# Seven products for eight in one more outgoing step of a split-precision feed-forward block

## The chip, the cores and the metric

The kernel runs on one core of a Trainium2 chip. Its time is that of one execution on the device, in microseconds (us), and the median of several executions is quoted. Numerical work is in float32. TensorE multiplies in a shortened float format (fp32r), so each factor is split into a high and a low part, and one product in full precision is three matmuls: high by high, high by low, low by high.

## The reference

One layer of a hybrid encoder on 512 tokens (T) of width 1024, from one conditioning vector c:

```python
x += 1/2 * g1 * SwiGLU_1(mod(RMSNorm(x)))
x += g2 * W_out( sig(gA) * W_A(WindowGQA+sink) + sig(gB) * W_B(DiffAttn) )
x += 1/2 * g3 * SwiGLU_2(mod(RMSNorm(x)))

def swiglu(h, w_in, w_out):
    gate, up = jnp.split(h @ w_in, 2, axis=-1)
    return (jax.nn.silu(gate) * up) @ w_out
```

The shifts, scales and gates (mod and g) are nine vectors of 1024, which come from c by the matrix w_mod (1024 by 9216). The hidden width of a SwiGLU is 2816, which is 22 chunks of 128. The first block ("first SwiGLU") is the one that the change touches most.

## The kernel before

The token axis lies along the free dimension, in two halves of 256; a chunk is 128 hidden units. Hidden chunks go in pairs, 0 to 10.

The first block's pairs 0 to 2 are computed by plain products. Each pair from 3 on is a `Unit` (u3 to u10): a 2x2 block product done with seven smaller products in place of eight, s1, s2, s3, s4, a11, a12 and a22. The weights' sums for that are formed on their way in, by transfers which GpSimd's queue adds to what lies in the buffer (`G.dma_start(..., accum_op=ALU.add)`); the sums of results are formed by VectorE and ScalarE from the PSUM banks, in `Unit.after`. A product of a unit is four steps deep, 24 matmuls of 256 columns, in `two` (L458 to L460). After s2, s1 and a11 a ScalarE COPY (L536) takes the bank out; the products that go on in that bank wait for it.

The outgoing product of the first block (hidden to model width) runs in four groups of chunks, `CHUNKS`: 0 to 6, 6 to 12, 12 to 16 and 16 to 22. Each is an `Out1`: eight rows, one for each 128 of the model width, and a row is (chunks in the group) x 3 matmuls of 512 columns in `mm3` (L174 to L176). After each row VectorE adds it to the residual x with the gate (L947, x_78 to x_85). Each row needs one weight load on SP's queue (`raw<-w1o`), and one split: a ScalarE CAST to the high part and a VectorE subtraction to the low part (both L190, `split_from`).

Between products the list `items1` places other work. `side1` runs modulation columns, one for each credit of 1.0, with 0.27 credited for each item: such a column is a load of 512 KB into one half of the buffer `room` (`b<-w_mod`) and a VectorE multiply-and-sum (L283, `b<-b,ka`). The second SwiGLU has its outgoing products done by sevens already (`act_split`, `out_unit`, with products of 18 matmuls of 256 columns in three parts of the depth): for that, the activations of a pair are also summed and split into seven operands.

Work on SP's and GpSimd's queues stands in the order of the program; PE, VectorE and ScalarE run in the order in which a list scheduler put them, and each engine takes its instructions strictly in turn. `tc.issue_after(i)` keeps an instruction behind i, `tc.high_priority()` moves one forward in that list.

After the first block come rows of constants (`row`: gains, lambda vectors, sinks), from which the rotary tables (L1104 to L1107), the lambda sums (L1088) and the sink copy are made, and then the mixer's norm: the last four rows of the final `Out1` are added (L947, then by token halves in L381), squared on ScalarE (L304), summed (L310) and reduced by small matmuls (`tp<-ones,f`, L343).

In the mixer's end the merged value is split to two parts for its outgoing product. The second SwiGLU begins with the unit `Plain`, whose gating is at L1765 to L1772.

Of the kernel before, what the change touches and what calls it, by code (L numbers as in the profile page):

```python
# [18 lines left out]
P = 128  # L19
# [93 lines left out]
EARLY, NEXT, SIDE, LATER = 3, 3, 0.27, 4  # L113
# [21 lines left out]
def layer(ctx: ExitStack, tc: tile.TileContext, a: dict):  # L135
# [326 lines left out]
    class Unit:  # L462
# [13 lines left out]
        asked, length = ("s1", "a11", "a12", "a22"), 1.0  # L476

        in_order, by_columns, asides = (), (), {}
# [148 lines left out]
    with tc.manual_schedule(engines=BOUND | {mybir.EngineType.SP, mybir.EngineType.Pool}):  # L627
# [246 lines left out]
    def in_post1(c, v, u):  # L874

        if c[1] == "1":
            u.v["g" + c[2]] = v
            S.activation(v, v, AF.Silu)
            if "c2" + c[2] in u.v:
                in_post1("c2" + c[2], u.v["c2" + c[2]], u)  # L880
            return
        if "g" + c[2] not in u.v:
            u.v[c] = v
            return
        g = u.v["g" + c[2]]
        V.scalar_tensor_tensor(g, g, -1.0, v, ALU.mult, ALU.mult)
        t, r = act_of(u.p), HALVES[int(c[2]) - 1]
        split_from(t[:, 0:2, r], t[:, 2:4, r], g.rearrange("p (j q) -> p j q", j=2))

    def in_unit1(p):  # L890
        srcs = {q: a["w1u"][p - PLAIN, i] for i, q in enumerate(("a11", "a12", "a21", "a22"))}
        u = Unit(srcs, 4, h1_operand, in_post1, p % 2)
        u.p, u.in_order = p, ('s2', 's4')
        if p == PLAIN:
            u.asides = {"s1": FIRST}
        elif 2 * p in [c.start for c in CHUNKS[1:]] or p == PLAIN + 1:
            u.asides = {"s2": FIRST}
        return u

# [54 lines left out]
    def item1(u, q, ks=None):  # L954
        items1.append((u, q, ks, side1))
# [15 lines left out]
    def side1(n=SIDE):  # L971
# [8 lines left out]
    with tc.manual_schedule(engines={mybir.EngineType.SP, mybir.EngineType.Pool}):  # L980
# [25 lines left out]
        begun = PLAIN  # L1006
        for n, chunks in enumerate(CHUNKS):


            final = n + 1 == len(CHUNKS)  # L1010
            for p in range(begun, max(chunks.stop // 2, PLAIN + 1)):
                u, nxt = units1[p], units1.get(p + 1)
                if p == PLAIN:
                    item1(u, "s1")
                    item1(u, "a11")
                elif p > begun:
                    item1(units1[p - 1], "a22")
                if p == PLAIN or p > begun:
                    item1(u, "a12")
                item1(u, "s2")  # L1020
                if nxt:
                    item1(nxt, "s1")
                item1(u, "s3")
                item1(u, "s4")
                if nxt:
                    item1(nxt, "a11")
            item1(u, "a22")
            if nxt:
                item1(nxt, "a12")
            begun, nxt = p + 1, nxt or u  # L1030
            out = Out1(chunks, "acc" if nxt.odd != final else "sc", final)
            if final:
                first = range(len(chunks) - 2)
                for m in range(2):
                    item1(out, m, first)
                for m in range(2):
                    item1(out, m, range(len(chunks) - 2, len(chunks)))
            for m in range(2 if final else 0, NC - LAST_1 if final else NC):
                item1(out, m)
# [9 lines left out]

    V.tensor_scalar(sub8, par[:, SUBLN : SUBLN + 1], 1.0 - LAM_INIT, None, ALU.mult)  # L1050
# [34 lines left out]
    lam_p = f2()[:, 0 : 2 * HD].rearrange("p (i d) -> p i d", i=2)  # L1085
    for i in range(2):
        o = ROW_LAM + 2 * i * HD
        V.tensor_tensor_reduce(  # L1088
            out=lam_p[:, i, :], in0=row[:, o : o + HD], in1=row[:, o + HD : o + 2 * HD],
            scale=1.0, scalar=0.0, op0=ALU.mult, op1=ALU.add, accum_out=lam_s[:, i : i + 1],  # L1090
        )
# [8 lines left out]
    for nm, o in (("qa", ROW_QA), ("ka", ROW_KA), ("qb", ROW_QB), ("kb", ROW_KB)):  # L1100
# [3 lines left out]
        V.tensor_tensor(C[:, :, 0:NF], cos_t, g0, ALU.mult)  # L1104
        V.tensor_tensor(C[:, :, NF:HD], cos_t, g1, ALU.mult)
        V.scalar_tensor_tensor(R[:, :, 0:NF], sin_t, -1.0, g1, ALU.mult, ALU.mult)
        V.tensor_tensor(R[:, :, NF:HD], sin_t, g0, ALU.mult)  # L1107
# [4 lines left out]
    V.tensor_copy(  # L1112
        sink.rearrange("p (g k) -> p k g", k=2), row[:, ROW_SINK : ROW_SINK + 8].rearrange("p (k g) -> p k g", k=2)
    )
# [575 lines left out]
    def main():  # L1690
# [24 lines left out]
        def then_b(j, g, y, r):  # L1715
# [3 lines left out]
            split_from(mh[j][:, r], ml[j][:, r], m)  # L1719
# [59 lines left out]
    act = {}  # L1779

    def act_operand(o, k):
        t = act[o, k]
        return t[:, 0, :], t[:, 1, :]

    places = []

    def act_place():

        if not places:
            t = spaces.pop(0)()  # L1790
            places.extend(t[:, i, :].rearrange("p (w q) -> p w q", w=2) for i in range(t.shape[1]))
        return places.pop(0)

    spaces = []

    def act_begin():
        act.clear()
        places.clear()
        spaces[:] = [b8] * 6 + [lambda: sbuf("ka", [P, 2, T], F32R, 1), u4]

    def act_split(u, k):

        ta, tb = f2(), f2()
        b = {f"b{n + 1}{t + 1}": u.v[f"g{t + 1}"][:, r] for t in range(2) for n, r in enumerate(HALVES)}
        b.update(n1=ta[:, T1], n2=ta[:, T2], t3=tb[:, T1], t4=tb[:, T2])
        for o in ("n1", "b11", "b21", "n2", "b22", "t3", "t4"):
            if o in SUMS:
# [305 lines left out]
```

## Time and profile before

| | us |
|---|---|
| median of 3 runs (1035.15 to 1036.81) | 1036.15 |
| the profiled execution | 1035.17 |
| its span, first to last instruction | 1033.4 |
| TensorE busy | 1027.9 (99%) |
| VectorE busy | 788.5 (76%) |
| ScalarE busy | 583.3 (56%) |

The page says of each engine how long it was busy in the span. Matmul rows overlap: each has a duration of 0.28 us for 256 columns, and the next begins 0.113 us later, so what a matmul costs is the step from start to start, which a window of known count gives. The stages of the first block that are spoken of below, by their starts on TensorE: group 0 to 6 from 107.6, group 6 to 12 from 178.45 to 211.13, group 12 to 16 from 249.29 to 271.08, the last group from 320.40. The granted clock of TensorE is 1.00 in the mean of the span, the level of 2.4 GHz.

### The profile page before, as it was taken

What the parts mean: (1) busy time and instruction counts of PE and PEld (TensorE: products, weight loads), DVE (VectorE), ACT (ScalarE), POOL (GpSimd) and SP (SyncE); (2) the same over time, 40 slices, a digit from 0 to 9 for tenths busy, and PEclk for the clock granted to TensorE, in tenths of its full rate; (3) what the DMA queues carried; (4) which work ended last, traced back from release to release, by engine and by line L of the source; (5) the groups of instructions that cost most, each with busy time, mean ns of one, the idle gap of its engine ahead of it and who ended that gap; (6) DMA issues with size and microseconds to landing.
All of it is one profiled execution on the core that took longest, in us unless ns stands there. A gap on an engine that the chain in (4) does not pass through costs nothing. (4 is left out here: it accounts for less than half of the span.)

```text
span 1033.4 us, 18849 instructions
## 1 busy us (share of the span) xinstructions
PE 1027.9 (99%) x7346; PEld 948.7 (92%) x7346; DVE 788.5 (76%) x1457; ACT 583.3 (56%) x1013; POOL 162.2 (16%) x189
## 2 busy tenths in 40 slices
PE   9999999999999999999999999999999999999998
PEld 7889899899998998899888888989999999999998
DVE  7886667567797679859772588976899777877877
ACT  6765335244455443668785856525867556655553
POOL 1101110111100100543323101001112112112210
PEclk9999999999999999999999999999999999999999
DMA  9977887967884369796737944974498998989974
GB/s 358 372 210 202 238 237 223 250 154 237 223 204 152 134 215 410 236 282 133 181 79 184 262 137 150 365 249 103 95 238 193 240 232 211 225 224 215 209 157 113
DMA packets 70233, 220.39 MB, mean 213 GB/s; under 512 B 8448, under 2 KB 13184, under 8 KB 70144
## 3 DMA queue, kind: packets, MB, share of 16 engines
q1 hardware_dynamic: 47808, 146.52, 39.2%
q0 software_dynamic: 19200, 68.17, 36.0%
q10 hardware_dynamic: 3136, 4.51, 1.2%
q8 instruction: 57, 0.93, 0.4%
q14 instruction: 32, 0.26, 0.1%
HBM read 208.94 MB, written 10.23 MB: 212 GB/s over the span
## 5 line engine op out<-in xcount | busy, mean ns | idle before, releaser
L190 ACT CAST high<-raw 128x1024 fp32r<-128x1024 f32 (+2 forms) x176 | 158.4, 914 | 152.0 <-PE sc L175 41.3
L190 DVE TENSOR_TENSOR low<-raw,high 128x1024 fp32r<-128x1024 f32 (+2 forms) x176 | 183.3, 1051 | 41.5 <-ACT high L190 40.1
L458 PE MATMUL acc<-b,high 128*128 128x256 f32 x508 | 140.9, 277 | 0.1
L459 PE MATMUL acc<-b,high 128*128 128x256 f32 x508 | 140.6, 277 | 0.1
L460 PE MATMUL acc<-b,low 128*128 128x256 f32 x508 | 140.6, 277 | 0.0
L460 PE MATMUL sc<-b,low 128*128 128x256 f32 x500 | 138.2, 276 | 0.0
L458 PE MATMUL sc<-b,high 128*128 128x256 f32 x500 | 138.1, 276 | 0.0
L459 PE MATMUL sc<-b,high 128*128 128x256 f32 x500 | 138.1, 276 | 0.0
L190 ACT CAST high<-u 128x1024 fp32r<-128x1024 f32 (+1 forms) x73 | 75.4, 1034 | 50.3 <-PE sc L175 20.2
L190 DVE TENSOR_TENSOR low<-u,high 128x1024 fp32r<-128x1024 f32 (+1 forms) x73 | 87.6, 1201 | 21.0 <-ACT high L190 19.4
L174 PE MATMUL sc<-b,high 128*128 128x512 f32 (+1 forms) x272 | 97.4, 358 | 0.0
L175 PE MATMUL sc<-b,high 128*128 128x512 f32 (+1 forms) x272 | 97.1, 357 | 0.0
L176 PE MATMUL sc<-b,low 128*128 128x512 f32 (+1 forms) x272 | 97.1, 357 | 0.0
L458 PEld LDWEIGHTS acc<-b,high 128*128 128x128 f32 x508 | 95.4, 188 | 0.6 <-ACT f L536 0.5
L459 PEld LDWEIGHTS acc<-b,high 128*128 128x128 f32 x508 | 95.4, 188 | 0.4 <-DVE b L1897 0.3
L460 PEld LDWEIGHTS acc<-b,low 128*128 128x128 f32 x508 | 95.4, 188 | 0.1
L458 PEld LDWEIGHTS sc<-b,high 128*128 128x128 f32 x500 | 93.9, 188 | 0.0
L459 PEld LDWEIGHTS sc<-b,high 128*128 128x128 f32 x500 | 93.9, 188 | 0.0
L460 PEld LDWEIGHTS sc<-b,low 128*128 128x128 f32 x500 | 93.9, 188 | 0.0
L174 PE MATMUL acc<-b,high 128*128 128x512 f32 (+1 forms) x240 | 89.1, 371 | 0.0
L176 PE MATMUL acc<-b,low 128*128 128x512 f32 (+1 forms) x240 | 86.6, 361 | 0.0
L175 PE MATMUL acc<-b,high 128*128 128x512 f32 (+1 forms) x240 | 86.5, 360 | 0.0
(397 smaller groups left out, 2716.3 us busy)
## 6 DMA issues: line engine op xcount, KB each, us to landing
u<-w_mod SPq DMA_DIRECT2D x38, 512.0 KB, 8.1
b<-w_mod SPq DMA_DIRECT2D x32, 512.0 KB, 5.5
raw<-w2i SPq DMA_DIRECT2D x31, 512.0 KB, 5.9
u<-w2i POOLq DMA_DIRECT2D x31, 512.0 KB, 7.1
raw<-w1u SPq DMA_DIRECT2D x24, 512.0 KB, 6.9
u<-w1u POOLq DMA_DIRECT2D x24, 512.0 KB, 6.5
raw<-w1o SPq DMA_DIRECT2D x24, 384.0 KB, 4.7
raw<-w_gate SPq DMA_DIRECT2D x16, 512.0 KB, 5.1
```

What stands on the lines that cost most here:

```text
L174: PE.matmul(out, wh, xh, start=first, stop=False)
L175: PE.matmul(out, wh, xl, start=False, stop=False)
L176: PE.matmul(out, wl, xh, start=False, stop=last)
L190: last = S.copy(hi, src), V.tensor_tensor(lo, src, f(hi), ALU.subtract)
L458: PE.matmul(out, wh[:, s], xh, start=first and j == 0, stop=False, skip_group_check=True)
L459: PE.matmul(out, wh[:, s], xl, start=False, stop=False, skip_group_check=True)
L460: PE.matmul(out, wl[:, s], xh, start=False, stop=last and j == 1, skip_group_check=True)
```

## The change

The second group of outgoing products (chunks 6 to 12, pairs 3, 4 and 5) is done by sevens: `SEVEN = (1,)`. It becomes two units, `out_unit1` with g = 0 and 1, each with seven products of depth three (18 matmuls of 256 columns). Its weights come from the same array in a new arrangement (`w1q`): eight loads of 384 KB on SP in place of eight, and eight more on GpSimd's queue that add to them. The activations of pairs 3 to 5 are summed and split to seven operands each (`act_split`, moved up from the second block) beside u4 to u6; those of u6 itself, which the third group needs, are split a little later (`eighth`). Units u4 to u6 and the two outgoing units have no modulation columns beside them; there are as many in all, at 0.75 for each row of an `Out1` and 0.3 for each product of the other units.

`row` is loaded beside u7 and no longer early; the tables, lambda sums and the sink copy that read it stand behind the last weight split ahead of the mixer (`issue_after(behind)`). The split of the merged value in the mixer is given a high priority. The unit `Plain` of the second block makes the four sums of its activations in a buffer of another pool (`aloft`: `b8` in place of two `f2`).

```diff
-EARLY, NEXT, SIDE, LATER = 3, 3, 0.27, 4
+SEVEN, RATES = (1,), (0.75, 0.3, 0.0)
+EARLY, NEXT, LATER = 3, 3, 4
...
-    row = u4(F32).rearrange("p a b -> p (a b)")[:, 0:NROW]
     small_loads = [
-        (row, a["row"].partition_broadcast(P)), (kept[0], a["pos"]), (freq, a["freq"].partition_broadcast(P)),
+        (kept[0], a["pos"]), (freq, a["freq"].partition_broadcast(P)),
     ]
...
         g = u.v["g" + c[2]]
+        if u.p in by_sevens:
+            V.tensor_tensor(g, g, v, ALU.mult)
+            return
         V.scalar_tensor_tensor(g, g, -1.0, v, ALU.mult, ALU.mult)
+        if u.p in by:
+            return
...
+    def act_split(u, k):
+        if u.aloft:
+            t = b8(F32)
+            ta, tb = t[:, 0, :], t[:, 1, :]
+        else:
+            ta, tb = f2(), f2()
+        b = {f"b{n + 1}{t + 1}": u.v[f"g{t + 1}"][:, r] for t in range(2) for n, r in enumerate(HALVES)}
+        b.update(n1=ta[:, T1], n2=ta[:, T2], t3=tb[:, T1], t4=tb[:, T2])
+        for o in ("n1", "b11", "b21", "n2", "b22", "t3", "t4"):
+            if o in SUMS:
+                sub(b[o], *(b[q] for q in SUMS[o]), o in NEGATED)
+            act[o, k] = t = act_place()
+            split_from(*t, b[o])
+            yield
...
+    def out_unit1(part, g, odd):
+        def post(c, v, u):
+            n, t = int(c[1]) - 1, int(c[2]) - 1
+            for j in range(2):
+                m = 4 * g + 2 * n + j
...
+                w = (less if n == 0 else modv[G1])[:, m : m + 1]
...
+                xr = x[m][:, HALVES[t]]
+                V.scalar_tensor_tensor(xr, v[:, j * H : (j + 1) * H], w, xr, ALU.mult, ALU.add)
+
+        r = slice((part.start - PLAIN) * 2 * P, (part.stop - PLAIN) * 2 * P)
+        srcs = {q: a["w1q"][g, i][:, r] for i, q in enumerate(("a11", "a12", "a21", "a22"))}
+        u = Unit(srcs, len(part), act_operand, post, odd)
+        return u
...
+    def load_row():
+        rows.append(u4(F32).rearrange("p a b -> p (a b)")[:, 0:NROW])
+        nc.sync.dma_start(rows[0], a["row"].partition_broadcast(P))
+
+    by[-1] = lambda: (iter(()), 0, load_row)
...
+            n = RATES[1 + (PLAIN in by_sevens and v.p == PLAIN + 1 or v.p - 1 in by_sevens or v not in units1.values())]
...
+            if nxt and not to:
+                item1(nxt, "s1", n=n)
+            for q in ("s3", "s4") if nxt else ("s4", "s3"):
+                item1(v, q, n=n)
+            if to:
+                item1(nxt, "s1", rest=True, n=n)
+            if nxt:
+                item1(nxt, "a11", n=n)
+            item1(v, "a22", n=n)
...
+    behind = split[1]
     for i in range(2):
         o = ROW_LAM + 2 * i * HD
-        V.tensor_tensor_reduce(
+        with tc.issue_after(behind):
+            V.tensor_tensor_reduce(
...
-        V.tensor_tensor(C[:, :, 0:NF], cos_t, g0, ALU.mult)
+        with tc.issue_after(behind):
+            V.tensor_tensor(C[:, :, 0:NF], cos_t, g0, ALU.mult)
...
-            split_from(mh[j][:, r], ml[j][:, r], m)
+            with tc.high_priority():
+                split_from(mh[j][:, r], ml[j][:, r], m)
...
     class Plain(Unit):
-        asked, more = ("a11", "a12", "a21", "a22"), {}
+        asked, more, aloft = ("a11", "a12", "a21", "a22"), {}, True
```

Three places in the order of the instructions bear on the steps below.

ScalarE, second group's outgoing products; before, casts of the rows' weights (768 columns) and the activations of u5 and u6:

```order
L190 CAST high<-raw_1635 128x768
L190 CAST high<-raw_1696 128x768
L190 CAST high<-raw_1727 128x768
L190 CAST high<-raw_1751 128x768
L190 CAST b_160_1630<-f_153_1453 128x2x256
L190 CAST high<-raw_1778 128x768
L878 ACTIVATE f_163_1665<-f_163_1665 128x512
L190 CAST high<-raw_1805 128x768
L190 CAST high<-raw_1829 128x768
```

ScalarE at the same place after the change; `sc_1895` and `acc_1999` are PSUM banks of the first and the second outgoing unit, and L539 is the COPY that was L536:

```order
L193 CAST high<-raw_1626 128x768
L539 COPY f_182_1914<-sc_1895 128x512
L193 CAST high<-u_162_1561 128x768
L193 CAST high<-raw_1861 128x768
L193 CAST high<-raw_1916 128x768
L539 COPY f_187_1992<-sc_1895 128x512
L193 CAST high<-u_170_1725 128x768
L539 COPY f_189_2018<-acc_1999 128x512
```

The COPYs now stand among the casts of the weights: a bank's COPY waits its turn behind the cast ahead of it.

VectorE, third group's rows, before; x_78 to x_81 are rows of the residual, L283 is a modulation column:

```order
L947 SCALAR_TENSOR_TENSOR x_78<-sc_2372,mod_90,x_78 128x512
L190 TENSOR_TENSOR low<-raw_2408,high 128x512
L947 SCALAR_TENSOR_TENSOR x_79<-sc_2392,mod_90,x_79 128x512
L190 TENSOR_TENSOR low<-u_183_1930,high 128x1024
L947 SCALAR_TENSOR_TENSOR x_80<-sc_2410,mod_90,x_80 128x512
L190 TENSOR_TENSOR low<-u_206_2369,high 128x1024
L947 SCALAR_TENSOR_TENSOR x_81<-sc_2428,mod_90,x_81 128x512
L190 TENSOR_TENSOR low<-raw_2426,high 128x512
L283 ISA b_80_573,mod_91<-b_80_573,ka_96,par 128x1024
L283 ISA mod_91 128x1
L947 SCALAR_TENSOR_TENSOR x_82<-sc_2454,mod_90,x_82 128x512
```

VectorE at the same rows after (L1066 was L947, L286 was L283):

```order
L1066 SCALAR_TENSOR_TENSOR x_78<-sc_2566,mod_90,x_78 128x512
L286 ISA b_80_573,mod_92<-b_80_573,ka_96 128x1024
L286 ISA mod_92 128x1
L193 TENSOR_TENSOR low<-raw_2600,high 128x512
L297 SCALAR_TENSOR_TENSOR mod_92<-mod_92,par,begin 128x1
L1066 SCALAR_TENSOR_TENSOR x_79<-sc_2584,mod_90,x_79 128x512
L193 TENSOR_TENSOR low<-u_194_2117,high 128x1024
L1066 SCALAR_TENSOR_TENSOR x_80<-sc_2605,mod_90,x_80 128x512
L193 TENSOR_TENSOR low<-u_219_2560,high 128x1024
L286 ISA b_80_573,mod_92<-b_80_573,ka_96 128x1024
L286 ISA mod_92 128x1
L1066 SCALAR_TENSOR_TENSOR x_81<-sc_2626,mod_90,x_81 128x512
```

Two columns now stand ahead of x_81's addition, where the first stood behind it.

VectorE, the end of the first block, before:

```order
L947 SCALAR_TENSOR_TENSOR x_80<-acc_3124,mod_90,x_80 128x512
L190 TENSOR_TENSOR u_274_3251<-raw_3249,u_273_3250 128x1024
L310 TENSOR_TENSOR f_248_3104<-f_248_3104,f_252_3144 128x512
L190 TENSOR_TENSOR low<-raw_3184,high 128x768
L947 SCALAR_TENSOR_TENSOR x_81<-acc_3148,mod_90,x_81 128x512
L1088 ISA f_261_3209,lam_s<-u_79_566 128x64
L1088 ISA lam_s 128x1
L1088 ISA f_261_3209,lam_s<-u_79_566 128x64
L1088 ISA lam_s 128x1
L190 TENSOR_TENSOR u_277_3257<-raw_3255,u_276_3256 128x1024
L310 TENSOR_TENSOR f_248_3104<-f_248_3104,f_254_3168 128x512
L381 SCALAR_TENSOR_TENSOR x_82<-sc_3263,mod_90,x_82 128x256
```

VectorE at the same place after; L1256 to L1259 make the tables (they were L1104 to L1107) and L1239 the lambda sums:

```order
L1256 TENSOR_TENSOR raw_3420<-u_273_3399,u_205_2308 128x4x32
L1257 TENSOR_TENSOR raw_3420<-u_273_3399,u_205_2308 128x4x32
L1066 SCALAR_TENSOR_TENSOR x_81<-acc_3355,mod_90,x_81 128x512
L1258 SCALAR_TENSOR_TENSOR raw_3420<-u_273_3399,u_205_2308 128x4x32
L1239 ISA f_274_3416,lam_s<-u_205_2308 128x64
L1239 ISA lam_s 128x1
L1239 ISA f_274_3416,lam_s<-u_205_2308 128x64
L1239 ISA lam_s 128x1
L1259 TENSOR_TENSOR raw_3420<-u_273_3399,u_205_2308 128x4x32
L1256 TENSOR_TENSOR raw_3420<-u_273_3399,u_205_2308 128x4x32
L313 TENSOR_TENSOR f_261_3311<-f_261_3311,f_267_3375 128x512
L1257 TENSOR_TENSOR raw_3420<-u_273_3399,u_205_2308 128x4x32
```

All sixteen table instructions, which stood ahead of x_78's addition, now lie around x_81's, ten ahead of it and six behind, and three of the splits `u<-raw,u` have moved behind the additions of x_82, x_83 and x_84.

## Rows read from the trace of the kernel before

**Rows 1.** The page's head, the span and each engine's busy time

```profile
span 1033.4 us, 18849 instructions
...
PE 1027.9 (99%) x7346; PEld 948.7 (92%) x7346; DVE 788.5 (76%) x1457; ACT 583.3 (56%) x1013; POOL 162.2 (16%) x189
```

**Rows 2.** Waits of TensorE in the whole span: us in total, times, longest

```profile
PE acc L634 <- DVE sm L640: 0.9, 1, 0.9
```

**Rows 3.** Windows by stage; busy time and (instructions) of each engine

```profile
core 0: us, PE busy (x) PEld busy (x) DVE busy (x) ACT busy (x) POOL busy (x), PEclk, DMA share, GB/s
178.45:211.13 32.68, 32.68 (x147) 27.04 (x145) 17.93 (x26) 7.13 (x8) 3.52 (x4) 1.00 0.91 258
249.29:271.08 21.79, 21.79 (x98) 18.03 (x97) 16.18 (x22) 6.73 (x9) 2.65 (x3) 1.00 1.02 288
271.08:273.88 2.80, 2.80 (x25) 2.80 (x24) 1.98 (x2) 1.02 (x1) 0.88 (x1) 1.00 1.02 415
837.75:854.07 16.32, 16.32 (x147) 16.32 (x145) 13.88 (x23) 7.86 (x12) 1.72 (x2) 1.00 1.00 232
```

**Rows 4.** Timeline around 764: start, duration, engine, line, operation

```profile
763.47 0.59 ACT L536 COPY f<-acc 128x512 f32<-128x512 f32 x1 [0.59 <-DVE f L1772]
...
763.73 0.28 PE L460 MATMUL sc<-b,low 128*128 128x256 f32 x1
...
764.11 0.39 PE L458 MATMUL acc<-b,high 128*128 128x256 f32 x1
...
764.33 0.28 PE L459 MATMUL acc<-b,high 128*128 128x256 f32 x1
```

**Rows 5.** VectorE by shape, 58 to 345: count, busy, mean ns, idle

```profile
L190 DVE TENSOR_TENSOR low<-raw,high 128x1024 fp32r<-128x1024 f32 x34 | 41.5, 1222 | 12.4 <-ACT high L190 11.6
...
L190 DVE TENSOR_TENSOR low<-raw,high 128x768 fp32r<-128x768 f32 x24 | 22.4, 952 | 6.6 <-ACT high L190 6.6
...
L947 DVE SCALAR_TENSOR_TENSOR x<-sc,mod,x 128x512 f32<-128x512 f32 x24 | 18.0, 750 | 27.2 <-PE sc L176 27.2
...
L283 DVE CUSTOM_DVE_ANT_0 b<-b,ka,begin 128x1024 f32<-128x1024 f32 x8 | 10.2, 1278 | 0.0
...
L190 DVE TENSOR_TENSOR low<-raw,high 128x512 fp32r<-128x512 f32 x8 | 5.3, 684 | 0.4 <-ACT high L190 0.4
```

**Rows 6.** ScalarE by shape, the same stretch

```profile
L190 ACT CAST high<-raw 128x768 fp32r<-128x768 f32 x24 | 19.3, 835 | 21.1 <-PE sc L175 11.4 <-DMA raw<-w1o 7.0 <-issue 1.2
...
L536 ACT COPY f<-acc 128x512 f32<-128x512 f32 x12 | 7.0, 582 | 3.7 <-PE acc L460 3.7
```

**Rows 7.** VectorE by shape, 790 to 1030

```profile
L190 DVE TENSOR_TENSOR b<-f,b 128x256 fp32r<-128x256 f32 x50 | 19.5, 420 | 1.3 <-ACT b L190 0.9
```

**Rows 8.** DMA issues: count, KB each, median us to landing

```profile
b<-w_mod SPq DMA_DIRECT2D x32, 512.0 KB, 5.5
...
u<-w2o POOLq DMA_DIRECT2D x6, 384.0 KB, 5.8
...
raw<-w1i SPq DMA_DIRECT2D x4, 512.0 KB, 11.0
```

**Rows 9.** Timeline before the mixer, three engines

```profile
323.84 0.28 DVE L1106 SCALAR_TENSOR_TENSOR raw<-u,u 128x128 f32<-128x128 f32 x1
...
324.05 0.28 DVE L1107 TENSOR_TENSOR raw<-u,u 128x128 f32<-128x128 f32 x1
...
336.95 0.75 DVE L947 SCALAR_TENSOR_TENSOR x<-acc,mod,x 128x512 f32<-128x512 f32 x1 [0.64 <-PE acc L176]
...
339.83 0.48 DVE L381 SCALAR_TENSOR_TENSOR x<-sc,mod,x 128x256 f32<-128x256 f32 x1
...
345.25 0.48 DVE L381 SCALAR_TENSOR_TENSOR x<-sc,mod,x 128x256 f32<-128x256 f32 x1 [0.59 <-PE sc L176]
...
345.83 0.42 ACT L304 ACTIVATE f<-x 128x256 f32<-128x256 f32 x1 [1.63 <-DVE x L381]
...
346.47 0.95 PE L343 MATMUL tp<-ones,f 128*128 128x2 f32 x8
```

More of the change, by code (lines that the diff above doesn't have):

```diff
@@ L898, in in_unit1, with act_operand, act_place, act_begin @@
         return u
+    act = {}
+    def act_operand(o, k):
+        return act[o, k]
+    places = []
+    def act_place():
+        if not places:
+            t = spaces.pop(0)()
+            places.extend((t[:, i, T1], t[:, i, T2]) for i in range(t.shape[1]))
+        return places.pop(0)
+    spaces = []
+    def act_begin(more=None):
+        act.clear()
+        places.clear()
+        spaces[:] = [b8] * 6 + [lambda: sbuf("ka", [P, 2, T], F32R, 1), u4]
+        if more is not None:
+            spaces[:] = [b8] * more + [u4]
+            for k in range(4):
+                places.append((hh[k][:, T2], hl[k][:, T2]))
@@ new lines, in layer, with seventh, piece, all_pieces @@
+    pending, by = [], {}
+    def seventh(u, k, begin):
+        return lambda: (act_split(u, k), 7, begin if k == 0 else None)
+    def piece():
+        if pending:
+            pending.pop(0)()
+    def all_pieces():
+        while pending:
+            piece()
+    def later_pieces(p):
+        steps, n, begin = by[p]()
+        if begin is not None:
+            all_pieces()
+            begin()
+        pending.extend([lambda: next(steps)] * n)
+    def along(*due):
+        def do():
+            for p in due:
+                later_pieces(p)
+            for _ in range(1 + (len(pending) > 7)):
+                piece()
+        return do
@@ new lines, in layer @@
+    by_sevens = [p for i in SEVEN for p in range(CHUNKS[i].start // 2, CHUNKS[i].stop // 2)]
+    less = small(NC)
+    def out_unit1(part, g, odd):
[3 more added lines that the diff above has]
+                m = 4 * g + 2 * n + j
+                while any((v, c) == (G1, m) for v, c, *_ in rest + asked):
+                    column(rest)
+                w = (less if n == 0 else modv[G1])[:, m : m + 1]
+                if n == 0 and m not in negated:
+                    negated.add(m)
+                    V.tensor_scalar(w, modv[G1][:, m : m + 1], -1.0, None, ALU.mult)
+                xr = x[m][:, HALVES[t]]
[4 more added lines that the diff above has]
+        return u
@@ L1005, in layer @@
             side1(1.0)
-        begun = PLAIN
+        order = [units1[PLAIN]]
         for n, chunks in enumerate(CHUNKS):
[L1010 to L1020, printed above, removed]
-                if nxt:
[L1022 to L1039, printed above, removed]
@@ new lines, in layer, with plain1 @@
+            order += [units1[p] for p in range(order[-1].p + 1, chunks.stop // 2)]
+            order[-1].then = chunks
+        def plain1(chunks, final, odd):
+            out = Out1(chunks, "acc" if odd != final else "sc", final)
+            first = range(len(chunks) - 2)
+            if final:
+                for m in range(2):
+                    item1(out, m, ks=first)
+                for m in range(2):
+                    item1(out, m, ks=range(len(chunks) - 2, len(chunks)))
+            for m in range(2 if final else 0, NC - LAST_1 if final else NC):
+                item1(out, m, n=RATES[0])
+            return out
@@ L1853, in layer @@
     plain = units[0] = Plain(units[0].srcs, 4, h_operand, None, 0)
+    for r in PARTS:
+        by.update({p: seventh(units[p], p - r.start, act_begin) for p in r})
     lead = units[1]
```

128 lines of the change are left out of this document (65 added, 63 removed).

## The prediction

> **What bounds the kernel.** I read the page's head first: TensorE is busy 1027.9 of 1033.4 us, VectorE 788.5 [rows 1]. Then the waits of TensorE: the view lists two, the longer of 0.9 us, both before the first block [rows 2]. So from the start of the first block on nothing but TensorE sets the time, and its windows tell the price of its work [rows 3]: busy time equals the window in each, at a granted clock of 1.00, the level of 2.4 GHz. A change can gain by taking columns off TensorE, or by closing small gaps that the view of waits doesn't list; it can lose where another engine comes late. Third, then, come the timeline for such gaps, the other engines' rows by shape for what the new work costs them, the DMA issues, and the end of the first block, where VectorE stands close to the path.
>
> **The change part by part.**
>
> *Outgoing products of group 6 to 12.* Removed are 8 rows of 18 matmuls of 512 columns: 144 in the window of 32.68 us, 226.9 ns each [rows 3]. Added are 2 units of 7 products of 18 matmuls of 256 columns: 252. The same form, 144 of them in the second block, takes 16.32 us, 113.3 ns each [rows 3]. 252 x 0.1133 = 28.56 us. The difference is 4.12 us, all on the path. Here I weigh a rule of the Trainium skill, "TensorE: Matmul & The Clock Gate", section "Wait — 56ns, not 53.3ns?": at the high clock every matmul costs its columns at 2.4 GHz and about 2.5 ns beside. By it (an estimate) 252 short ones take 27.5 us, 144 long ones 31.1 us, and the gain is only 3.6 us. The windows don't agree: twice 113.3 is 226.7, against 226.9, so there is no fixed part to pay twice, and I keep 4.12. One window goes slower than that: the product at 271.08 took 2.80 us for 24 matmuls [rows 3], 116.7 ns each. Were all 252 so slow, 252 x 0.0034 = 0.86 us would be lost; I take 0.1 for a unit or so of it and keep 0.9 as an end.
>
> *VectorE and ScalarE beside it.* From u4's second product to the end of the two new units TensorE has 20 products of 24 matmuls and the 252: 732 of 0.1133, 83.0 us. VectorE's instructions there, by the order: 40 on 256 columns at 0.42 [rows 7], 23 on 512 at 0.684, 21 splits of 1024 at 1.222, 14 of 768 at 0.952, one column at 1.278 [rows 5]: 16.8 + 15.7 + 25.7 + 13.3 + 1.3 = 72.8 us, 88%. In the second block VectorE is busy 13.88 of 16.32 us beside the same kind of product, 85%, and TensorE has no gap [rows 3]. The mean fits, then; what decides is the chains. In an outgoing unit the longest is on ScalarE: a cast of 768 columns, 0.835, that may start only when the product before has let its weights go, and behind it the COPY of the bank, 0.582 [rows 6]. Together 1.42 us, in a window of one product of 18 matmuls, 2.04 us: 0.6 us over. The transfers that add to the weights land in 5.8 us [rows 8], against the 10.2 us of five products from one to the other's use. Cost taken: 0. Ends: 0, and 14 products in each of which the COPY comes 0.2 us late, 2.8 us. A gain has no place here, since nothing waits there before.
>
> *Fewer columns early, more in the third group.* With 0.75 for each row, one column falls on 3.63 us (2.72 / 0.75; a row of twelve 512-column matmuls is 21.79 / 8 [rows 3]). From the first row to the last but one VectorE has 8 additions of 0.750, 3 splits of 0.684, 4 of 1.222, and 4 columns of 1.278 [rows 5]: 6.0 + 2.1 + 4.9 + 5.1 = 18.1, near 19 us with the small instructions, in 21.79. Before it was 16.18 [rows 3]. The banks rotate by three, so an addition may come 2 rows, 5.4 us, late. Cost 0; the case in which the transfers of the columns are slow is a rival below. The columns taken away beside u4 to u6 leave room and give nothing, since nothing waits.
>
> *Constants and tables behind the last split.* At the end of the first block ten table instructions now stand ahead of x_81's addition, six behind it. Two neighbours start 0.21 us apart [rows 9]. Ten are 2.1 us; the split `u<-raw,u` of 1.22 has left that place, and 0.64 us were idle ahead of x_81 [rows 9]: x_81 comes 2.1 - 1.22 - 0.64 = 0.2 us late. Behind it six tables (1.3) and the sink copy (0.2) come in, another split of 1.22 goes out: 0.3 more, half a microsecond at x_82. Then the three splits lie among the additions: a round is an addition of 0.48 [rows 9], a split of 1.22 [rows 5] and a sum on 256 columns, 0.42 as that of [rows 7]; each starts about 0.07 before the end of the one ahead, as the table instructions do [rows 9]. That is 1.91 us, three rounds 5.7, where x_82 to x_85 took 5.42, from 339.83 to 345.25 [rows 9]. So x_85 comes some 0.8 us later than at 345.25, and its square, which ended at 345.83 + 0.42 = 346.25, ends at 347.0 or so. The small matmuls that read it begin at 346.47, eight of them in some 0.8 us [rows 9]; the first four need only the sum, so the last square is needed at 346.9. Cost 0 to 0.3, and I take 0.15. The ends are 0, and 1.0 where the cast of a late split holds a square up as well.
>
> *`aloft`.* In `Plain` the COPY on ScalarE starts at 763.47, after an idle 0.59 that VectorE's L1772 ended, and TensorE's first matmul into that bank begins at 764.11, 0.38 us after the one before it at 763.73; the next follows after 0.22 [rows 4]. With 0.113 as the step, (0.38 - 0.113) + (0.22 - 0.113) = 0.37 us are lost. After the change the four sums no longer take the buffer that this COPY waits for; the order has it waiting for TensorE alone. Gain 0.37; ends 0 (the COPY waits for something that is released as late) and 0.4.
>
> *Split of the merged value ahead.* TensorE has no wait in the mixer [rows 2], so it can't gain. Cost 0.
>
> **Sum.** 1033.4 - 4.12 - 0.37 + 0.10 + 0.15 = 1029.2 us of span. The profiled execution took 1035.17, 1.77 beside its span: 1030.9. The median of the runs lies 0.98 above the profiled execution, so the forecast is **1031.9**.
>
> **Rivals.**
>
> *A, the forecast.* All hides but 0.15: 1031.9. With either the end of the slow step (0.9) or that of the tables (1.0) above, and below with 0 for what I took and 0.7 for what the runs differ among themselves, its own range is 1031.0 to 1033.0. For it: equal load without a gap in the second block.
>
> *B, the outgoing units wait.* The margin of the COPY is 0.6 us a product. A split or an adding transfer that is late by more than that costs TensorE the rest, each time. With 0.2 us in 10 of the 14 products it is 2 us: 1033.9. For it: VectorE's 88% is over the 85% that has been seen to do; ScalarE takes the casts and COPYs in turn. Against it: the weights are due several products ahead, and TensorE had no wait in the second block.
>
> *C, slower: columns crowd the third group.* The buffer has two halves. A half is free when its multiply has ended, 1.28 us, and full when the next transfer has landed. At a landing of 5.5 us [rows 8] a round is 6.8 us for two halves, 3.4 a column, which fits in the 3.63. The additions stand behind the columns in VectorE's row, so if the transfers are slower, x_79 and those behind it wait, and TensorE waits for banks once the 5.4 us of slack are gone. It starts to lag at a landing of 6.0 and, over six columns, decides where the lag goes over 5.44: (landing + 1.28) / 2 - 3.63 = 0.91, a landing of 7.8; it takes the whole gain of 4.1 at 9.2. At the 11.0 us that `raw<-w1i` took at the start [rows 8], it is 6.14 - 3.63 = 2.51, times 6 is 15.1, less 5.4 is 9.6 us: 1041.5. For it: the DMA share is 1.02 in that group already [rows 3]. Against it: the 32 column loads of the trace have a median of 5.5, though that queue's loads wait in turn there too.
>
> *D, no effect.* Were the 256-column matmuls paced by something other than columns in this place, say by loading weights, which was busy for the whole of 16.32 us beside them [rows 3], the gain could shrink to the 0.4 of `aloft`: 1035.6. Against it: that same window has them at 113.3 ns.
>
> **How the numbers follow.** A 0.68, B 0.18, C 0.08, D 0.06. The range reaches from just under A's lower end, 1030.9, past B's 1033.9 to 1035.0, where B's worst case (2.8 us) ends; C and D, 0.14, are left out. A measurement here tells 0.2%, 2.1 us, from no change: faster is below 1034.1. That is all of A and half of B, and a bit of C: 0.78. Within 0.2%, to 1038.2: the rest of B, D and a third of C: 0.14. Slower: the rest of C and what I don't see: 0.08.
>
> **What would show it.** Right: a window of the two outgoing units of 28.6 us with TensorE busy all of it; no step over 0.2 us at the first matmul into `acc` in `Plain`; the first small matmul `tp<-ones` without an idle over 0.3. B is shown by waits `sc<-.. <- ACT f L539`, C by `DVE <- DMA b<-w_mod` and additions that lag TensorE by more than two rows. The prediction is wrong if the span lies above 1031 or the new units take more than 29.5 us.

## The result and the profile after

The changed kernel takes 1040.65 us in the median of seven executions (1038.81 to 1045.58), the kernel before 1035.15: a ratio of 1.0048, with a 95% interval of 1.0035 to 1.0062 (the two medians divide to 1.0053, inside it). It is slower by 0.5%, where 0.4% less was forecast. The profile is that of the slowest of the seven executions, 1045.58; what it shows is read for places, and sizes are taken from the experiments below.

The page's head, as in [rows 1]:

```profile
span 1043.8 us, 19173 instructions
...
PE 1031.3 (99%) x7454; PEld 956.3 (92%) x7454; DVE 804.2 (77%) x1508; ACT 592.9 (57%) x1040; POOL 169.1 (16%) x197
```

TensorE is busy for only 3.4 us more than before, in a span that is 10.4 us longer. The view of its waits, which listed two in the kernel before, the longer of 0.9 us [rows 2], both ahead of the first block, now has five more entries beside that one:

```profile
PE acc L461 <- ACT f L539: 3.9, 2, 2.9
PE acc L461 <- DVE f L541: 1.3, 1, 1.3
PE acc L637 <- DVE sm L643: 0.9, 1, 0.9
PE acc L179 <- DVE low L193: 0.9, 1, 0.9
PE acc L463 <- DVE low L193: 0.7, 1, 0.7
PE tp L463 <- DVE low L193: 0.6, 1, 0.6
```

The first block's new outgoing units are not where they are. The timeline of TensorE shows the first two, the longest among them, between the products s2, s4 and s3 of u6, ahead of the units:

```profile
181.01 0.28 PE L462 MATMUL acc<-b,high 128*128 128x256 f32 x1
182.03 0.39 PE L463 MATMUL acc<-b,low 128*128 128x256 f32 x1 [0.74 <-DVE low L193]
...
182.49 0.28 PE L463 MATMUL acc<-b,low 128*128 128x256 f32 x1
185.62 0.39 PE L461 MATMUL acc<-b,high 128*128 128x256 f32 x1 [2.85 <-ACT f L539]
...
187.48 0.41 PE L461 MATMUL acc<-b,high 128*128 128x256 f32 x1
```

At 182.03 a product waits for the low part of its weights, at 185.62 s3 waits for the COPY of the bank that s2 has left. By steps from start to start, the six waits of the first block (ending at 182.03, 185.62, 289.92, 293.77, 322.75 and 327.07) cost 0.90, 3.02, 1.46, 0.79, 1.23 and 1.02, together 8.4 us. They cost more than themselves, as the windows around the longest show (columns as in [rows 3]):

```profile
core 0: us, PE busy (x) PEld busy (x) DVE busy (x) ACT busy (x) POOL busy (x), PEclk, DMA share, GB/s
184.00:186.00 2.00, 0.38 (x3) 0.38 (x4) 1.31 (x3) 2.00 (x4) 0.00 (x0) 1.00 0.75 294
186.00:188.00 2.00, 2.00 (x15) 2.00 (x14) 2.00 (x5) 1.19 (x3) 0.87 (x1) 0.68 0.02 8
188.00:190.00 2.00, 2.00 (x11) 2.00 (x11) 0.55 (x2) 0.83 (x1) 0.00 (x0) 0.50 0.98 138
...
192.00:212.00 20.00, 20.00 (x173) 20.00 (x172) 14.00 (x19) 9.94 (x14) 5.24 (x6) 1.00 0.87 200
305.00:313.00 8.00, 8.00 (x71) 7.92 (x70) 6.31 (x9) 2.80 (x4) 0.88 (x1) 1.00 0.95 227
```

TensorE stood for most of 184 to 186. In 188 to 190 the granted clock is 0.50, the level of 1.2 GHz, and 11 matmuls take the time of 18. From 186.84 to 190.04 the step is 0.213 us, 15 steps, 1.5 us lost. After that the clock is 1.00 again, but 20 us hold 173 matmuls, where 20 us of the outgoing units in experiment 9 below hold 179: the step is 117.8 ns in place of 113.3, and it stays so until the third group begins at 252.98. From 305 to 313 it is 113.3. I call a step of some 117.8 ns at full clock a slow step. There are 533 in a row from 190.20, 68 from 294.00 and 385 from 773.07; what they cost over the kernel before, with the scattered ones, is 4.6 us. The sum is -4.1 + 8.4 + 1.5 + 4.6 = 10.4, the difference of the spans. Smaller terms are left out and nearly cancel: 1.0 for a second longer step behind each wait, -0.4 of `aloft`, -0.3 at the start of the program.

Why the COPY is late stands on ScalarE. Its timeline from 174:

```profile
174.22 0.84 ACT L193 CAST high<-u 128x768 fp32r<-128x768 f32 x1 [5.40 <-DMA u<-w1q]
...
177.00 0.58 ACT L539 COPY f<-acc 128x512 f32<-128x512 f32 x1
177.47 1.05 ACT L193 CAST high<-raw 128x1024 fp32r<-128x1024 f32 x1
178.42 1.05 ACT L193 CAST high<-u 128x1024 fp32r<-128x1024 f32 x1
...
183.28 0.63 ACT L880 ACTIVATE f<-f 128x512 f32<-128x512 f32 x1 [1.84 <-DVE f L546]
...
184.26 0.83 ACT L193 CAST high<-raw 128x768 fp32r<-128x768 f32 x1
184.99 0.58 ACT L539 COPY f<-acc 128x512 f32<-128x512 f32 x1
```

ScalarE stood 5.4 us, until a transfer that adds to the weights of the first outgoing unit (`u<-w1q`) had landed. That cast isn't needed before the unit begins, but it stands in ScalarE's row ahead of the casts of u6's weights. Those are late by as much (178.42), so VectorE's low parts are, and its sum at 182.56, for which the ACTIVATE at 183.28 waits; behind that stands a cast, and behind it the COPY at 184.99 that TensorE waits for. The transfer had been issued late, on GpSimd's queue, whose timeline is:

```profile
164.65 0.88 POOL L516 DMA_DIRECT2D raw<-w1u  x1 [12.03 <-DVE low L193]
165.20 1.23 POOL L497 DMA_DIRECT2D u<-w1q  x1
```

Its own load had long been asked for on SP (at 148.98), but on GpSimd's queue it stood behind an adding transfer of u6 that waited 12 us for a buffer.

### The profile page after: what moved, and what is told of

The parts are those of the page before. It is cut to its first block, busy times and chain, and to the rows that moved or that the text cites. A ratio compares the mean times of both kernels' runs of the same rounds, so it can differ in the third digit from the quotient of the medians.

```text
span 1043.8 us, 19173 instructions
## 1 busy us (share of the span) xinstructions
PE 1031.3 (99%) x7454; PEld 956.3 (92%) x7454; DVE 804.2 (77%) x1508; ACT 592.9 (57%) x1040; POOL 169.1 (16%) x197
## 4 chain that ended last, share of the span: by engine, by line
PE 87%; DMA 5%; DVE 3%; issue 2%; ACT 1%; SPq 0%; POOL 0%; DVEq 0%; ACTq 0%; POOLq 0%
PE acc L462 6%; PE acc L461 6%; PE acc L463 6%; PE sc L462 6%; PE sc L463 6%; PE sc L461 6%; PE acc L177 5%; PE acc L179 5%; PE acc L178 5%; PE sc L178 3%; PE sc L177 3%; PE sc L179 3%; DMA u<-w1u 3%; PE tp L1433 2%; PE sc L190 2%
## 5 line engine op out<-in xcount | busy, mean ns | idle before, releaser
L461 PE MATMUL acc<-b,high 128*128 128x256 f32 x542 | 151.7, 280 | 5.2 <-ACT f L539 3.9
L463 PE MATMUL acc<-b,low 128*128 128x256 f32 x542 | 151.4, 279 | 0.7 <-DVE low L193 0.7
L462 PE MATMUL acc<-b,high 128*128 128x256 f32 x542 | 151.2, 279 | 0.1
L463 PE MATMUL sc<-b,low 128*128 128x256 f32 x534 | 148.1, 277 | 0.0
L461 PE MATMUL sc<-b,high 128*128 128x256 f32 x534 | 148.1, 277 | 0.0
L462 PE MATMUL sc<-b,high 128*128 128x256 f32 x534 | 148.0, 277 | 0.0
L461 PEld LDWEIGHTS acc<-b,high 128*128 128x128 f32 x542 | 102.8, 190 | 6.2 <-ACT f L539 4.3
L463 PEld LDWEIGHTS acc<-b,low 128*128 128x128 f32 x542 | 102.7, 190 | 1.0 <-DVE low L193 0.9
L462 PEld LDWEIGHTS acc<-b,high 128*128 128x128 f32 x542 | 102.5, 189 | 0.4 <-DVE b L2019 0.3
L461 PEld LDWEIGHTS sc<-b,high 128*128 128x128 f32 x534 | 100.6, 188 | 0.1
L463 PEld LDWEIGHTS sc<-b,low 128*128 128x128 f32 x534 | 100.5, 188 | 0.1
L462 PEld LDWEIGHTS sc<-b,high 128*128 128x128 f32 x534 | 100.2, 188 | 0.0
L177 PE MATMUL sc<-b,high 128*128 128x512 f32 (+1 forms) x224 | 78.7, 351 | 0.0
L178 PE MATMUL sc<-b,high 128*128 128x512 f32 (+1 forms) x224 | 78.5, 350 | 0.0
L179 PE MATMUL sc<-b,low 128*128 128x512 f32 (+1 forms) x224 | 78.4, 350 | 0.0
```

The source lines that it names most:

```text
L177: PE.matmul(out, wh, xh, start=first, stop=False)
L178: PE.matmul(out, wh, xl, start=False, stop=False)
L179: PE.matmul(out, wl, xh, start=False, stop=last)
L461: PE.matmul(out, wh[:, s], xh, start=first and j == 0, stop=False, skip_group_check=True)
L462: PE.matmul(out, wh[:, s], xl, start=False, stop=False, skip_group_check=True)
L463: PE.matmul(out, wl[:, s], xh, start=False, stop=last and j == 1, skip_group_check=True)
```

## Experiments

Each experiment was timed beside its own runs of the kernel before, whose median lay between 1035.2 and 1036.5 us. So kernels of different experiments are compared here by their ratios to the kernel before, and not by their medians.

**1. The cast of the outgoing units' first weights later.** In `out_unit1`:

```diff
+        u.in_order = ("s1",)
```

> The changed kernel with one edit: the cast of the first product's weights of each outgoing unit stands behind the last COPY of a bank (in ScalarE's row it moves from 4 places ahead, past one ACTIVATE, one CAST and one COPY). Theory Q (ScalarE's queue): in the changed kernel this cast held ScalarE for 5.4 us until the sum of the weights had landed at 174.2, and the waits of TensorE that end at 182.03 (0.9 us) and 185.62 (3.0 us) come from that; so both shrink to under 1 us together, and the median falls by 3 to 5 us, to some 1036. Theory L (load: VectorE and ScalarE have too much to do beside the sevens): the waits stay, within a microsecond, and the median stays at 1039 to 1041. The waits at 289.92, 293.77, 322.75 and 327.07 stay by both.

1038.5 us, ratio 1.0028 (1.0017 to 1.0038). Of the waits at u6 one is left, 2.56 us (it was 3.0) ending at 184.14, with a cast of u6's that waits 2.4 us for its own adding transfer, which is issued behind that of the outgoing unit on the same queue. The ratio fell by 0.20%, half of what theory Q asked for: to move the cast helps ScalarE, and the queue of transfers is as late as before.

**2. The weights of the outgoing units asked for earlier.** In the same place:

```diff
+        u.ASK = dict(u.ASK, s1=12)
```

> The changed kernel with one edit: the first product's weights of each outgoing unit are asked for 12 products ahead in place of 9, so that their adding transfer stands on GpSimd's queue ahead of one that waits 12 us for a buffer of u6's weights. Theory Q: the sum lands before ScalarE comes to its cast, the 5.4 us of ScalarE are gone, and with them the waits at 182.03 and 185.62 (3.9 us); median 3 to 5 us lower, some 1036. Theory L: no change within 1 us, 1039 to 1041.

1035.77, ratio 1.0001 (0.9990 to 1.0012): 0.47% less than the changed kernel's, 4.9 us. The adding transfer is now issued at 152.64, ahead of the one that waits:

```profile
152.64 1.22 POOL L497 DMA_DIRECT2D u<-w1q  x1
164.99 0.87 POOL L516 DMA_DIRECT2D raw<-w1u  x1 [11.12 <-DVE low L193]
```

and ScalarE's cast of it, at 169.80, no longer waits for it. Theory Q holds for most of it, theory L is out: the load is the same. Of the 3.9 us at u6, a COPY 1.2 us late at 183.15 is left, and of the later waits 1.1 and 0.9 us at 313.98 and 318.23.

**3. No columns in the third group's rows.**

```diff
-SEVEN, RATES = (1,), (0.75, 0.3, 0.0)
+SEVEN, RATES = (1,), (0.75, 0.5, 0.0)
...
-                item1(out, m, n=RATES[0])
+                item1(out, m, n=0.0 if chunks.start == 12 else RATES[0])
```

> The changed kernel with the modulation columns taken out of the third group's rows (credit 0 there) and 0.5 in place of 0.3 beside each product of the units that have columns; their number is the same. Theory C (crowding: the columns' transfers in the third group slow the weights' transfers down, so that the sum for u9 lands only at 286.2 and holds ScalarE for 6.9 us): the waits at 289.92 and 293.77, 2.2 us together, go to under 0.5, and the median falls by 1.5 to 4 us; those at 182.03 and 185.62 stay. Theory Q' (the order of the queues alone, whatever the columns do): the waits stay within 0.5 us and the median stays at 1039 to 1041.

1041.12, ratio 1.0052 (1.0040 to 1.0064). The waits at 289.92 and 293.77 are gone, as theory C had it, but the time isn't lower: the wait of 3.0 at u6 is there with its half clock and 530 slow steps, and one of 1.5 has come at 98.73, beside a unit that has more columns now: VectorE's column there stands 3.5 us until its transfer has landed, with low parts behind it. Near the end of the block 0.9 us are left, at 325.84. Inconclusive by itself.

**4. The sums of `Plain` alone, on the kernel before.** In `act_split`:

```diff
-        ta, tb = f2(), f2()
+        if u is plain:
+            t = b8(F32)
+            ta, tb = t[:, 0, :], t[:, 1, :]
+        else:
+            ta, tb = f2(), f2()
```

> The kernel before with one part of the change alone: the four sums of the unit Plain in a buffer of the other pool. Expected: the gap ahead of 764.11 (0.37 us) gone and nothing else moved; 0.3 to 0.4 us less, within the spread of the runs. If the COPY waits for something else as late, no gap is closed and the time stays.

1035.23, ratio 1.0001 (0.9991 to 1.0010). The gap of [rows 4] is gone: the COPY starts 0.87 us earlier, at 762.60, without a wait, and TensorE's step into `acc` is as any other:

```profile
763.87 0.28 PE L460 MATMUL sc<-b,low 128*128 128x256 f32 x1
763.98 0.28 PE L458 MATMUL acc<-b,high 128*128 128x256 f32 x1
764.10 0.28 PE L459 MATMUL acc<-b,high 128*128 128x256 f32 x1
```

0.37 us can't be told in the time, and the span is the same, since the start of the program took 0.5 longer in this execution.

**5. All of the change but the sevens.** `SEVEN = ()`, with the columns where the change has them:

```diff
-SEVEN, RATES = (1,), (0.75, 0.3, 0.0)
+SEVEN, RATES = (), (0.75, 0.3, 0.0)
...
-            n = RATES[1 + (PLAIN in by_sevens and v.p == PLAIN + 1 or v.p - 1 in by_sevens or v not in units1.values())]
+            n = RATES[1 + (v.p in (4, 5, 6))]
...
-                item1(out, m, n=RATES[0])
+                item1(out, m, n=0.0 if chunks.start == 6 else RATES[0])
...
-            if v.p - 2 in by_sevens and v.p - 1 not in by_sevens and v in units1.values():
+            if v.p == 7 and v in units1.values():
```

> The changed kernel without its main part: the second group's outgoing products by eight again (144 matmuls of 512 columns), with everything else of the change, and the columns where the change has them (none beside u4 to u6 and the second group). Theory Q (the waits come from the queues' order in the sevens' own stage and are handed on from there): no wait at 182 to 186, and none in the third and the last group; 1033.4 - 0.4 of span, a median within 0.1% of the kernel before. Theory R (the rest of the change, above all the columns left for the third and the last group, makes the later waits): about 2 to 4.5 us of waits stay between the third group's rows and the last group's, and the median is 2 to 4 us above the kernel before, 1037.5 to 1039.5.

1039.5, ratio 1.0036 (1.0023 to 1.0049). Theory R: without the sevens there are waits at 238.53, 288.32, 296.72, 316.92 and 320.98, 3.2 us, and none at u6. The view of SP's waits from 230 to 320 shows what is behind them:

```profile
SPq L248 <- DVE mod L286: 65.9, 12, 15.0
SPq L1032 <- DVE low L193: 15.2, 7, 7.3
```

A column's load (L248) waits until VectorE has freed its half of the buffer, and every weight load behind it on SP's queue waits too: 65.9 us in twelve times. One such load is that of the first weights of u9 (`u<-w1u`), and the timelines show what comes of it:

```profile
260.99 0.33 SPq L248 DMA_DIRECT2D b<-w_mod  x1
261.41 0.74 SPq L495 DMA_DIRECT2D u<-w1u  x1
...
271.37 0.87 POOL L497 DMA_DIRECT2D u<-w1u  x1 [10.18 <-DMA u<-w1u]
...
280.76 1.05 ACT L193 CAST high<-u 128x1024 fp32r<-128x1024 f32 x1 [5.13 <-DMA u<-w1u]
```

The column's load had waited 5.1 us for its half; the weights' load follows it, the adding transfer waits for that load, and ScalarE stands 5.1 us before the cast of the sum. The same chain stands in the changed kernel, with 6.9 us of ScalarE at 286.22. From its first plain product (58.06) to the first small matmul of the mixer's norm, the first block is 4.0 us longer than in the kernel before. In this profile, the slowest of eight, 4.1 us more are slow steps, 915 in a row from 822.90 in the second block, right behind a wait of 0.5 us.

**6. As 5, with even columns.** 0.27 for every product and row:

```diff
-SEVEN, RATES = (), (0.75, 0.3, 0.0)
+SEVEN, RATES = (), (0.27, 0.27, 0.27)
...
-                item1(out, m, n=0.0 if chunks.start == 6 else RATES[0])
+                item1(out, m, n=RATES[0])
```

> No sevens in the second group, and even columns (0.27 throughout): of the change only the later row of constants, the tables behind the last split, the priority of the merged value's split and the sums of Plain are left. Without sevens but with the change's columns the median was 0.36% above the kernel before. Theory R (the columns' place made that): it goes back to the kernel before, within 0.1%. If the tables, the priority or the row made it, it stays 0.25% or more above.

1035.12, ratio 0.9994 (0.9986 to 1.0003), and no wait of TensorE over 0.3 us in the first block. The same view of SP:

```profile
SPq L1032 <- DVE low L193: 34.6, 10, 7.7
SPq L248 <- DVE mod L286: 28.0, 4, 12.7
```

28.0 us in four times in place of 65.9. All waits of SP together are not much shorter, 76.1 us against 84.6; what differs is which loads stand behind them. The load of u9's first weights and its adding transfer are issued at

```profile
253.96 0.42 SPq L495 DMA_DIRECT2D u<-w1u  x1
...
260.98 1.06 POOL L497 DMA_DIRECT2D u<-w1u  x1
```

7.5 us earlier than in 5 at the load, and ScalarE doesn't wait for the sum. Slower transfers, the rival explanation, are the smaller part: the load took 6.4 us here and 9.4 in 5, the adding transfer 10.6 here and 9.3 in 5. So the place of the columns is what made experiment 5 slow, 0.42% or 4.4 us, and the later row, the tables, the priority and `aloft` together cost nothing that can be told.

**7. The earlier asking, and s4 ahead of s3.**

```diff
+        u.ASK = dict(u.ASK, s1=12)
...
-            for q in ("s3", "s4") if nxt else ("s4", "s3"):
+            for q in ("s3", "s4") if nxt and not to else ("s4", "s3"):
```

> The changed kernel with the earlier asking (12 for 9) and one more edit: where an outgoing unit follows, the product s4 stands ahead of s3, so that the 24 matmuls of s4 lie between s2 and s3, which work in one bank, and not 6. The wait of 1.24 us that ends at 183.15 with the earlier asking alone is the COPY of that bank, behind a cast. Theory Q: it goes, 0.8 to 1.2 us, and the median falls from 1035.8 to some 1034.8. If it is the chain of ScalarE as a whole that is late, the wait only moves to a later product and the median stays at 1035.8.

1035.31, ratio 0.9994 (0.9982 to 1.0007), 0.07% under experiment 2, which is inside the intervals. The wait at u6 is gone; those at 312.66 and 317.33 stay, 0.4 and 1.2 us.

**8. As 7, with even columns** (`RATES = (0.27, 0.27, 0.27)`).

> As the one before (earlier asking, s4 ahead of s3), and the modulation columns spread evenly again, 0.27 for every product and row, so that they stand beside u4 to u6 and the outgoing units too, and end earlier. Theory R (the columns kept for the third and last group make the waits there, 1.1 and 0.9 us at 314 and 318): these go, the median falls by another 1.5 to 2.5 us to some 1032.5 to 1033.5, unless the columns make waits beside u4 to u6 in their place. Theory Q: these waits come from a weight sum that lands late whatever the columns do, and stay; no change, or slower by what the columns cost VectorE beside the sevens (88% busy without them).

1034.83, ratio 0.9990 (0.9979 to 1.0001). The waits of the third and last group are gone, but one of 0.5 us has come at 223.89 and one of 1.9 us at 233.86, with half clock behind it. ScalarE's timeline, and SP's:

```profile
230.81 1.05 ACT L193 CAST high<-raw 128x1024 fp32r<-128x1024 f32 x1 [6.32 <-DMA raw<-w1u]
...
233.23 0.57 ACT L539 COPY f<-sc 128x512 f32<-128x512 f32 x1
```

```profile
217.21 0.44 SPq L1008 DMA_DIRECT2D u<-row  x1
217.75 0.43 SPq L495 DMA_DIRECT2D raw<-w1u  x1
```

The load of u7's weights is issued right behind the row of constants and lands 13 us later; for 6.3 us ScalarE stands before its cast.

**9. As 8, with the row of constants beside u8.**

```diff
-            if v.p - 2 in by_sevens and v.p - 1 not in by_sevens and v in units1.values():
+            if v.p == 8 and v in units1.values():
```

> The kernel with the earlier asking, s4 ahead of s3 and even columns, and the row of constants loaded beside u8 in place of u7. There one wait was left, 1.9 us at 233.86, with 1.7 us of half clock around it: ScalarE's cast of a weight load of u7 stood 6.3 us, until the load had landed 13 us after its issue right behind the row of constants. Theory Q (a load that lands late holds ScalarE's queue): with the row elsewhere the wait and its half clock go, 2 to 3.6 us, the span comes to 1029.4 to 1031, the median to 1031 to 1033. If it was the crowd of all loads there, the wait stays within 0.5 us and the median at 1034.8.

1032.79, ratio 0.9975 (0.9965 to 0.9985): faster than both kernels, than the kernel before by 0.25%. In the first block one wait is left, 1.2 us by the step, and the outgoing units go at the fast step:

```profile
PE tp L463 <- DVE low L193: 1.0, 1, 1.0
```

```profile
188.00:208.00 20.00, 20.00 (x179) 20.00 (x178) 18.54 (x31) 10.85 (x15) 5.30 (x6) 1.00 1.02 265
```

**10. Columns between both** (as 8, `RATES = (0.4, 0.27, 0.13)`, the row beside u7).

> Earlier asking, s4 ahead of s3, and the columns between both: 0.4 for each row, 0.27 beside units, 0.13 beside u4 to u6 and the outgoing units; the row of constants beside u7. Theory R (columns late make waits in the third and last group, columns early make them beside the sevens): both sorts are smaller than with 0.75 / 0 or 0.27 throughout, 1 to 2 us of waits in all, median 1033 to 1034.5. If the waits have nothing to do with where the columns stand, 1035.

1036.96, ratio 1.0012 (1.0002 to 1.0022): waits of 1.7 at 185.58, 1.4 at 226.72, 0.4 and 1.0 at 315 and 319. By its ratio theory R's middle way is above either end (0.9994 in 7, 0.9990 in 8), though its interval overlaps that of 7. In this profile another 1.7 us are slow steps, 190 from 227.06 and 195 from 787.16. Which load now stands behind which I did not follow.

**11. As 9, with u7's weights asked for earlier.** In `in_unit1`:

```diff
+        if p == 7:
+            u.ASK = dict(u.ASK, s1=11, a11=10, a12=8)
```

> The fastest version so far (earlier asking for the outgoing units, s4 ahead of s3, even columns, the row of constants beside u8) with u7's weights asked for two products earlier, so that two of their loads stand on SP's queue ahead of a column's load that waits for its half of the buffer. One wait was left there, 1.19 us at 225.51, behind a cast of u7's weights that had waited 3.6 us for its transfer. Theory Q: the wait goes, and the median falls by 1 to 1.5 us, to some 1031.5. If the transfers are slow by their number and not by their place in the queue, the wait stays or moves, and the median with it, 1032.8.

1034.87, ratio 0.9989 (0.9981 to 0.9998), not faster than 9. The wait there is 1.45 us now, and one of 1.0 has come at 184.26. A miss; why the wait at 226 stays is open. The waits are not all of it: in the second block, which the edit leaves alone, slow steps run from 740.16 to 808.23, 2.6 us in this profile. Windows of 11 and then of 9:

```profile
740.20:808.20 68.00, 68.00 (x579) 68.00 (x579) 61.69 (x98) 47.07 (x79) 13.49 (x16) 1.00 0.93 212
```

```profile
740.20:808.20 68.00, 68.00 (x600) 68.00 (x601) 63.81 (x100) 47.76 (x79) 13.89 (x16) 1.00 0.96 220
```

So the difference of 9 and 11 can't be put down to the loads alone.

**12. Even columns and the later row, without 7's two edits.**

> The changed kernel with even columns (0.27) and the row of constants beside u8, but neither the earlier asking nor s4 ahead of s3. If the two causes add up (the columns' place, and the order of the queues at u6), the waits of the third and last group are gone and the one between u6's s2 and s3 stays, 3 us and what follows it: 0.3% above the kernel before at most, 1035 to 1038. If the columns were the one cause, it is as fast as the fastest version, 1032.8.

1039.74, ratio 1.0039 (1.0025 to 1.0053): the waits of 0.9 and 3.2 us at u6 are back, with their half clock, and those of the last group stay away. The two causes add up within the noise: 0.9975 and the 0.54% that 7 takes off the changed kernel give 1.0029, inside the interval, near its lower end. The even columns and the later row alone take only 0.09% off the changed kernel, inside the noise, and 0.19% where u6 is mended (7 against 9). The median is 1.7 us over the range expected.

## Why the prediction was wrong

*The matmuls.* Right. At the fast step of experiment 9, 252 take 28.6 us. From the first plain product to the first small matmul of the mixer's norm, the first block takes 287.98 us in experiment 6 (58.50 to 346.48), without the sevens, and 285.09 in experiment 9 (59.15 to 344.24), with them and a wait of 1.19: without the wait the gain is 4.1 us, against the 4.12 of the sum. In the ratios of these two it is 0.19%, 2.0 us, the wait included. (From 5 to 7 the ratio falls by 0.42%, 4.3 us, but both have waits of their own, and that they cost about the same is luck.) The prediction weighed a rule of the Trainium skill, a fixed part of about 2.5 ns per matmul ("TensorE: Matmul & The Clock Gate", section "Wait — 56ns, not 53.3ns?"). It is not borne out: with 226.9 ns for 512 columns [rows 3] and 113.3 for 256 there is none to be seen. What I had as an end, a slow step of 116.7 ns, was 117.8 for 63 us.

*VectorE and ScalarE beside it, cost 0.* This step failed. I weighed mean load (88%) and the margin of a COPY in the outgoing units, and both held: there is no wait inside those units. I did not ask at which cast ScalarE would come to stand still. The landing time of 5.8 us was set against 10.2 us of products, but the clock of that transfer starts at its place in GpSimd's queue, not when its buffer is asked for: it was issued at 165.20, 16 us after its load, and landed 8.9 us later, at 174.1. The landing was mis-sized by 3.1 us, and the 16 us ahead of it were not in the working at all. Waits of 3.9 us at u6 came of it, of which earlier asking takes 2.7, and with half clock and slow steps some 5 (experiment 2); with the order of s3 and s4 mended too it is 0.54%, 5.6 us (7). Rival B named a late adding transfer; its place (inside the units) and price (2 us) were wrong. The product that has no cover is seen in the timeline, too: only six matmuls stand between s2 and s3.

*More columns in the third group, cost 0.* This failed as well. With the sevens undone it costs 4.4 us (5 against 6); beside the sevens it is worth less in the ratios, 0.09 to 0.19% (12), so u6 is the larger part of the changed kernel's loss. Rival C had the place and the sign; its mechanism was wrong, and that its dearest case, 1041.5, lies near the 1040.65 measured is luck. It followed the columns' own round through the buffer and VectorE's additions, and those had room: the latest addition starts 2.5 us after its row's end, with 5.4 to spare. What counts is what stands behind a column on SP's queue. A load that waits for its half of the buffer holds all weight loads after it, and ScalarE then stands before the casts.

*Tables behind the last split, 0.15.* Right, it costs nothing: the first small matmul starts at 355.68, with no step over that of its neighbours:

```profile
355.56 0.28 PE L179 MATMUL sc<-b,low 128*128 128x256 f32 x1
355.68 0.95 PE L346 MATMUL tp<-ones,f 128*128 128x2 f32 x8
356.48 0.37 PE L177 MATMUL sc<-b,high 128*128 128x256 f32 x1
```

*`aloft`, -0.37.* Right in the trace, too small for the time. *Split of the merged value:* no wait, as said.

*The sum.* With the waits away but one of 1.2 us, the span is 1030.9 in experiment 9; the forecast of 1029.2 and that wait make 1030.4. The terms on TensorE's path were right, and two zeros were not. Beside that, two of the prediction's small sums are off: the chances named for "within 0.2%" add up to 0.18 and not 0.14, and rival D's price by its own terms is 1035.8 and not 1035.6.

## What to carry to other kernels

Where one engine is 99% busy, ask of each added transfer not how long it takes but what stands ahead of it on its queue, and which engine comes to stand before it: an early cast of data that is late stops everything behind it. Work that is moved to "where there is room" takes its place in every in-order queue along; here a buffer wait of a side task held the main task's loads. Don't take a wait of a saturated engine at its own length alone: behind the wait of 3.0 us here, 1.5 us went to the half clock and 2.4 to slow steps.

## What the runs showed of the hardware

A wait of TensorE of 3 us was followed by a granted clock of 0.50, 1.2 GHz, from 186.8 to 190.0, and then by a step of 117.8 ns in place of 113.3 at full clock, for 62.8 us. In experiment 5 there were 915 such steps in a row behind a wait of 0.5 us, with no half clock ahead of them, and in the changed kernel 385 from 773.07 and in experiment 11 579 from 740.16 with no wait of 0.2 us right ahead. In experiment 12 a wait of 3.2 us, with half clock behind it, left none in the profiled execution, the fastest of its six. What decides it, no run here shows. The seven executions of the changed kernel lie 6.8 us apart, the eleven of experiment 6 only 1.5; whether slow steps make up that spread is not shown, since each kernel has one profile.
